# State-space decays: the causal mask added by VectorE, and growth read from the spread sums

## The chip, the cores and the metric

The kernel runs on one core of a Trainium2 chip. The metric is the device time of one execution in microseconds (us), the median of several runs. The engines work side by side, each through its own queue in a fixed order, and wait for one another on semaphores: TensorE (PE, products into PSUM; its weight loads are PEld), VectorE (DVE), ScalarE (ACT), GpSimd (POOL) and SyncE (SP), which issues most of the transfers.

## What is computed

One layer of a hybrid decoder for 336 tokens (256 new prompt tokens, 64 sampled tokens of 8 sequences, 16 meta tokens): a gated convolution branch and a state-space (SSD) branch that share one input projection, then a mixer that picks experts. The change touches the SSD branch alone, and there these two lines:

```python
acs = jnp.cumsum(dtc * Ag, axis=1)
seg = acs[:, :, None] - acs[:, None, :]
decay = jnp.exp(jnp.where(causal[None, :, :, None, None], seg, -jnp.inf))
...
y_diag = jnp.einsum('btsgr,bsgrp->btgrp', cb[..., None] * decay, dx)
y_off = jnp.einsum('btgn,bgrpn->btgrp', Cc, hc) * jnp.exp(acs)[..., None]
```

`decay` is a masked exponential of differences of running sums, for each of 32 heads; `exp(acs)` is what is called growth below.

## The kernel before

The input projection is 80 blocks of 128 output rows. Each block (`pj`) is 24 products of 320 or 336 columns: 16 with the rounded weights `wh` (made by ACT, L243) and 8 with the remainder `wl` (made by POOL, now and then by DVE, L247). The 32 heads form 8 groups `g` of four. While PE works through the projections of group g+1, the state-space work of group g (`ssd`) is let in between them, a step after each projection. PE's products are pinned to program order (`mm`, `tr`); DVE, ACT and POOL are put in order by a scheduler, except that all ACT functions that need a table are chained in program order (`chain`).

Four tiles of PSUM matter. Tag `y` has two buffers and holds in turn `pdec` (running sums of one head, spread over 128 partitions), and later `py` and `po` (the outputs). A `pdec` can be written only when the tile two before it has been read. Tag `pb` (one buffer) holds `pcv`, the sum of the long convolution: 31 taps, each one DVE instruction on 256 columns and one on 64 (L509), put at low priority so that they fill DVE's free time. Tag `pj` has three buffers, `misc` two.

In a group, `ssd` runs in steps. First `decay(0)`, `decay(1)`; after a projection `turn(0)` (transposes `ptr`, copied by ACT L643 and scaled by DVE L644 into `xt`), `decay(2)`, `decay(3)`; after the next `turn(1)`, `turn(2)`, `growth(0)`, `growth(1)`; then `inner` (L657, scores times decay), states and outputs. `update` adds to the sampled states `st` (L709) and stands just ahead of the next group's `decay(0)`. `gated` turns a projection into the convolution's input: a sigmoid on ACT (`xnf`, L219), then DVE writes `ccat` (L591 to L593), then ACT starts the sum `pcv` (L507), then DVE's taps begin.

A decay before: PE spreads the sums of head h by a product with a column of `id3`, adds the mask `mneg` by a second product with an identity, and ACT takes the exponential in three pieces, since the bias (minus the sum at the row) differs between them. Growth is spread again, two heads side by side on 64 partitions each, and ACT takes its exponential into `e2`.

Of the kernel before, what the change touches and what calls it, by code (L numbers as in the profile page):

```python
# [7 lines left out]
F32 = mybir.dt.float32  # L8
F32R = mybir.dt.float32r
BF = mybir.dt.bfloat16  # L10
# [3 lines left out]
AF = mybir.ActivationFunctionType  # L14
OP = mybir.AluOpType
# [8 lines left out]
T = TP + NQ * TS  # L24
NB_IN = 80
H = 32
# [9 lines left out]
T2 = 320  # L36
# [122 lines left out]
def body(tc, ia, oa, stop=None):  # L159
    nc = tc.nc  # L160
    with ExitStack() as top:
# [13 lines left out]
        def mm(*a_, **kw):  # L175
            i_ = nc.tensor.matmul(*a_, **kw)  # L176
            if pin[0]:
                tc.keep_in_program_order(i_)
# [28 lines left out]
        def C(name, rows=128):  # L207
            o, n = CST[name]
            if o < NCK:
                return cst[:rows, o:o + n]  # L210
            return cstm[0][:rows, o - NCK:o - NCK + n] if o < NCM else cstm[1][:rows, o - NCM:o - NCM + n]
# [228 lines left out]
        def step_sizes():  # L440
# [33 lines left out]
            act(el, p3, AF.Exp)  # L474
            acs.extend(at_[:, i] for i in range(3))
            wd.extend(wt_[:, i] for i in range(3))
            acs3 = mp.tile([3 * H, T], BF, name="acs3", tag="acs3")
            stack3(acs3, pT, H, dp, "r1")
            id3 = mp.tile([3 * H, H], BF, name="id3")
            keep(nc.vector.tensor_copy(id3, C("sel32", 3 * H)))  # L480
            mneg = mp.tile([128, T], BF, name="mneg")
            keep(nc.vector.tensor_copy(mneg, mnf))
            identb = mp.tile([128, 128], BF, name="identb")
            keep(nc.vector.tensor_copy(identb, ident))
            fixed.extend((acs3, id3, mneg, identb))
            yield

        MCAT = MC + TP + NQ * (MC + TS)
# [121 lines left out]
        def ssd(g, xg, bc, sz):  # L610
# [8 lines left out]
            def decay(r):  # L619
                h = 4 * g + r  # L620
                pb = ps.tile([128, T], F32, name="pdec", tag="y", bufs=2)[:, :T2]
                mm(pb, id3[:, h:h + 1].to_broadcast([3 * H, 128]), acs3[:, :T2], start=True, stop=False)
                mm(pb, identb, mneg[:, :T2], start=False, stop=True)
                for i, (t0, L) in enumerate(OTILES):
                    act(dec[:, r, t0:t0 + L], pb[:, t0:t0 + L], AF.Exp, bias=acs[i][:, h:h + 1])

            def growth(b):
                pb = ps.tile([128, T], F32, name="pdec", tag="y", bufs=2)[:, :T2]
                for r in range(2):
                    h = 4 * g + 2 * b + r  # L630
                    mm(pb[r * 64:(r + 1) * 64], id3[:, h:h + 1].to_broadcast([3 * H, 64]), acs3[:, :T2],
                       start=True, stop=True)
                act(e2[:, b], pb, AF.Exp)

            def decay_b(q):
                return el[:, q, 4 * g:4 * g + 4, None].to_broadcast([128, 4, P])
# [82 lines left out]
            yield  # L719
            turn(1)  # L720
            turn(2)
            growth(0)
            growth(1)
            for s_ in range(2):
                nc.scalar.copy(cz[:, 4 * s_:4 * s_ + 4, 8 * s_:8 * s_ + 8],
                               CT[:, SQ + 32 * s_:SQ + 32 * s_ + 32].rearrange("p (q t) -> p q t", q=4))
# [34 lines left out]
        def gnorm_stats():  # L761
            r8 = tp.tile([128, T], F32, name="rs", bufs=2)[:G, :T2]
            rstd_of(r8, pgn, 256, tp, load=False)
            r24 = mp.tile([3 * H, T], BF, name="acs3", tag="acs3")[:, :T2]
            nc.vector.memset(r24, 0.0)
            stack3(r24, r8, G, tp, "yo")
            return r24

        def gnorm(g, r24):
            p = ps.tile([128, T], F32, name="pgb", tag="y", bufs=2)[:, :T2]  # L770
            mm(p, id3[:, g:g + 1].to_broadcast([3 * H, 128]), r24, start=True, stop=True)
            for b in range(2):
                y = ygf[g][:, b, :T2]
                nc.vector.scalar_tensor_tensor(y, y, V("m_norm", 2 * g + b), p, op0=OP.mult, op1=OP.mult)
# [87 lines left out]
        for n, f in enumerate(conf(0) + zsteps[:1] + steps + zsteps[1:]):  # L862
            f()
            if n in (1, 4, 5):
                run(old, 1)
        acs3, id3, mneg, identb = fixed
        dt_scope.close()
        sp = ls.enter_context(tc.tile_pool(name="sp", bufs=1))

# [783 lines left out]
```

## Time and profile before

| | |
|---|---|
| median of 3 runs | 1304.52 us (1301.46 to 1305.58) |
| the profiled execution | 1300.87 us, its span 1299.1 us |
| instructions | 23902 |
| DVE, ACT, POOL busy | 74%, 41%, 46% of the span |
| products `pdec` with `acs`, `id` / with `mneg`, `identb` | 64 / 32 |
| ACT exponentials `dec` from `pdec` / `e` from `pdec` | 96 / 16 |
| first and last `pdec` product | 54.1 and 348.0 us |

In a timeline row stand the start in us, the duration, the engine, the line, the operation, output and input with the size, how many, and in brackets the idle time of the engine ahead of it with what ended it. Rows of several instructions give the time from the first start to the last end; each instruction's own duration overlaps the next by about 0.1 us on DVE and ACT and by half on PE, so costs are taken from starts. The view of windows gives for each stretch the busy time of PE, PEld, DVE, ACT and POOL with counts, then the granted TensorE clock, the DMA share and GB/s.

### The profile page before, as it was taken

To read this page: it belongs to the slowest core of one execution; us is meant where nothing else is said; L and a number is where in the kernel's file an instruction comes from. 1 tells how busy PE (TensorE), PEld (TensorE's weight loads), DVE (VectorE), ACT (ScalarE), POOL (GpSimd) and SP (SyncE) were. 2 spreads that over 40 slices of the span, in tenths; PEclk is the share of its full clock that TensorE was granted. 3 is DMA by queue.
4 is the path that set the end of the run, shared out by engine and by line. 5 is a ranking of instruction groups with operands and counts; after the bars stand their busy time and mean duration, and the time that the engine had idled before them with its cause. 6 is when DMAs were issued, how large, how long until landed. Compare 5 with 4: busy or idle time off the path is not lost.

```text
span 1299.1 us, 23902 instructions
## 1 busy us (share of the span) xinstructions
PE 1270.9 (98%) x9015; PEld 1223.2 (94%) x9015; DVE 956.2 (74%) x2240; ACT 529.6 (41%) x1395; POOL 592.9 (46%) x552
## 2 busy tenths in 40 slices
PE   9999999999989999999999899999999999999997
PEld 7998988999889999999999889999999999999997
DVE  7888778878887235549999968688788888545444
ACT  6787877888766444544232212212110110100102
POOL 2487777877774666974132223223332322122210
PEclk9899999999999999999999989999999999999999
DMA  6435453454433444766989999999999999999992
GB/s 246 165 126 185 155 191 134 156 186 167 149 129 136 146 149 153 254 231 221 382 328 416 416 414 415 414 412 408 413 414 415 415 415 414 402 414 415 405 414 88
DMA packets 85907, 373.80 MB, mean 288 GB/s; under 512 B 10000, under 2 KB 15376, under 8 KB 66208
## 3 DMA queue, kind: packets, MB, share of 16 engines
q1 hardware_dynamic: 48336, 166.82, 34.5%
q0 software_dynamic: 19584, 142.62, 26.9%
q10 hardware_dynamic: 17872, 62.84, 12.1%
q8 instruction: 71, 1.16, 0.4%
q14 instruction: 44, 0.36, 0.1%
HBM read 359.18 MB, written 13.06 MB: 287 GB/s over the span
## 4 chain that ended last, share of the span: by engine, by line
PE 83%; DVE 7%; DMA 6%; ACT 3%; issue 1%; POOL 1%; ACTq 0%; DVEq 0%
PE pj L176 32%; PE va L1517 25%; PE pj L1415 17%; DMA wuv<-in_peer_uv_dram,gid 3%; DMA eraw<-in_uT_dram 3%; PE pg L1443 1%; PE pst L176 1%; DVE ygat L1313 1%; PE po L176 1%; DVE wuv L1303 1%; PE pdec L176 1%; PE psc L1193 1%; PE py L176 1%; DVE pcv L509 1%; DMA wdt<-in_w_dt_dram 1%
## 5 line engine op out<-in xcount | busy, mean ns | idle before, releaser
L1147 POOL DMA_INDIRECT wuv<-in_peer_uv_dram,gid x136 | 173.0, 1272 | 484.7 <-PE va L1517 149.6
L247 POOL TENSOR_TENSOR wl<-wraw,wh 128x1024 fp32r<-128x1024 f32 (+1 forms) x160 | 279.6, 1760 | 117.1 <-ACT wh L243 68.8
L1517 PE MATMUL va<-S,eraw 128*128 128x184 f32 x2048 | 325.4, 320 | 0.0
L1517 PEld LDWEIGHTS va<-S,eraw 128*128 128x128 f32 x2048 | 318.9, 190 | 0.9 <-issue 0.9
L1415 PE MATMUL pj<-nd,eraw 128*128 128x184 f32 x1792 | 294.5, 324 | 9.9 <-DMA eraw<-in_uT_dram 8.1
L1415 PEld LDWEIGHTS pj<-nd,eraw 128*128 128x128 f32 x1792 | 282.8, 192 | 11.3 <-issue 9.0
L1313 DVE SCALAR_TENSOR_TENSOR ygat<-wuv,scg,ygat 128x1024 f32<-128x1024 f32 x128 | 164.1, 1282 | 108.1 <-ACT scg L1308 108.0
L176 PE MATMUL pj<-ah,wh 128*128 128x336 f32 (+1 forms) x768 | 242.5, 326 | 0.3 <-ACT xnf L219 0.3
L176 PE MATMUL pj<-al,wh 128*128 128x336 f32 (+1 forms) x768 | 232.2, 315 | 0.0
L1305 ACT ACTIVATE scg<-scg 128x1 f32<-128x1 f32 x136 | 27.3, 202 | 398.0 <-DVE wuv L1303 220.4
L1303 DVE SCALAR_TENSOR_TENSOR wuv<-wuv,x2m 128x1024 f32<-128x1024 f32 x128 | 156.2, 1220 | 17.3 <-DMA wuv<-in_peer_uv_dram,gid 17.0
L509 DVE SCALAR_TENSOR_TENSOR pcv<-ccat,vec,pcv 128x256 f32<-128x256 f32 x464 | 150.1, 389 | 17.1 <-ACT pcv L507 17.1
L243 ACT CAST wh<-wraw 128x1024 fp32r<-128x1024 f32 x125 | 131.2, 1050 | 73.4 <-PE pj L176 54.0
L176 PEld LDWEIGHTS pj<-ah,wh 128*128 128x128 f32 x768 | 145.4, 190 | 6.3 <-issue 2.0
L176 PEld LDWEIGHTS pj<-al,wh 128*128 128x128 f32 x768 | 145.0, 190 | 0.8
L176 PE MATMUL pj<-ah,wl 128*128 128x336 f32 (+1 forms) x768 | 137.2, 314 | 0.3 <-POOL wl L247 0.3
L176 PEld LDWEIGHTS pj<-ah,wl 128*128 128x128 f32 x768 | 119.8, 188 | 0.7 <-POOL wl L247 0.6
L1417 ACT ACTIVATE S<-pj 128x184 f32<-128x184 f32 x128 | 38.8, 318 | 128.0 <-PE pj L1415 127.7
L523 DVE SCALAR_TENSOR_TENSOR pj<-mcat,vec,pj 128x360 f32<-128x360 f32 x96 | 57.0, 595 | 0.6 <-ACT pj L521 0.6
L1454 DVE SCALAR_TENSOR_TENSOR S<-pg,S 128x232 f32<-128x232 f32 (+1 forms) x92 | 34.7, 420 | 29.8 <-PE pg L1443 29.6
L219 ACT ACT_TABLE_LOAD x38 | 48.8, 1283 | 0.7
L1415 PE MATMUL pj<-nd,pre 128*128 128x184 f32 x256 | 42.0, 319 | 0.0
(387 smaller groups left out, 1694.7 us busy)
## 6 DMA issues: line engine op xcount, KB each, us to landing
wraw<-in_w_in_dram SPq DMA_DIRECT2D x80, 512.0 KB, 3.3
eraw<-in_vE_dram SPq DMA_DIRECT2D x64, 512.0 KB, 9.5
eraw<-in_vE_dram ACTq DMA_DIRECT2D x64, 512.0 KB, 9.4
eraw<-in_uT_dram SPq DMA_DIRECT2D x60, 512.0 KB, 9.2
eraw<-in_uT_dram ACTq DMA_DIRECT2D x52, 512.0 KB, 9.9
st<-in_state_dram SPq DMA_DIRECT2D x8, 1024.0 KB, 6.9
out_ssm_s_dram<-st SPq DMA_DIRECT2D x8, 1024.0 KB, 6.3
wraw<-in_w_mo_dram SPq DMA_DIRECT2D x16, 512.0 KB, 3.2
```

The source lines that it names most:

```text
L176: i_ = nc.tensor.matmul(*a_, **kw)
L219: i_ = nc.scalar.activation(out, in_, f, **kw)
L243: (nc.vector.tensor_copy if on_dve else nc.scalar.copy)(h, src)
L247: (nc.gpsimd if on_pool else nc.vector).tensor_tensor(l[:, q:q + m], src[:, q:q + m], h[:, q:q + m].bitcast(F32), op=OP.subtract)
L509: t = nc.vector.scalar_tensor_tensor(o, i_, wv, a_, op0=OP.mult, op1=OP.add)
L523: nc.vector.scalar_tensor_tensor(o, cat[:, w:w + n], wv, o, op0=OP.mult, op1=OP.add)
L1147: i_ = nc.gpsimd.indirect_dma_start(out=u, out_offset=None, in_=ia["peer_uv"], in_offset=bass.IndirectOffsetOnAxis(ap=gid[:, c:c + 1], axi ...
L1303: nc.vector.scalar_tensor_tensor(u[:, :D], u[:, :D], 1.0, x2m if c < NPICK else x2e, op0=OP.mult, op1=OP.mult, accum_out=w)
L1313: nc.vector.scalar_tensor_tensor(a_, u[:, D:], scg[:, c:c + 1], a_, op0=OP.mult, op1=OP.add)
L1415: i_ = nc.tensor.matmul(p[:, :ND], raw[:, k, :], nd[:, k, :], start=(k == 0), stop=(k == KD - 1))
L1417: nc.scalar.activation(Sv(b), p[:, :ND], AF.Gelu)
L1517: i_ = nc.tensor.matmul(va[k // 2][:, k % 2], raw[:, k, :], Sv(b), start=(b == 0 and k % 2 == 0), stop=(b == 127), skip_group_check=True)
```

## The change

The product with the mask goes, and `identb` with it. DVE adds the bias and the mask in one instruction for each of the three pieces (from `pdec` in PSUM to `dec` in SBUF, without the exponential). ACT takes growth, the exponential of the sums alone, from 64 partitions of the same `pdec`, and after each second head one exponential over both heads of `dec`, in place. `growth` and its products go. `id3` and `acs3` get 128 rows instead of 96, the added ones zero.

```diff
-            acs3 = mp.tile([3 * H, T], BF, name="acs3", tag="acs3")
+            acs3 = mp.tile([128, T], BF, name="acs3", tag="acs3")
+            nc.gpsimd.memset(acs3[3 * H:], 0.0)
             stack3(acs3, pT, H, dp, "r1")
-            id3 = mp.tile([3 * H, H], BF, name="id3")
-            keep(nc.vector.tensor_copy(id3, C("sel32", 3 * H)))
+            id3 = mp.tile([128, H], BF, name="id3")
+            keep(nc.vector.tensor_copy(id3, C("sel32")))
...
-            identb = mp.tile([128, 128], BF, name="identb")
-            keep(nc.vector.tensor_copy(identb, ident))
-            fixed.extend((acs3, id3, mneg, identb))
+            fixed.extend((acs3, id3, mneg))
...
             def decay(r):
                 h = 4 * g + r
                 pb = ps.tile([128, T], F32, name="pdec", tag="y", bufs=2)[:, :T2]
-                mm(pb, id3[:, h:h + 1].to_broadcast([3 * H, 128]), acs3[:, :T2], start=True, stop=False)
-                mm(pb, identb, mneg[:, :T2], start=False, stop=True)
+                mm(pb, id3[:, h:h + 1].to_broadcast([128, 128]), acs3[:, :T2], start=True, stop=True)
                 for i, (t0, L) in enumerate(OTILES):
-                    act(dec[:, r, t0:t0 + L], pb[:, t0:t0 + L], AF.Exp, bias=acs[i][:, h:h + 1])
-
-            def growth(b):
-                pb = ps.tile([128, T], F32, name="pdec", tag="y", bufs=2)[:, :T2]
-                for r in range(2):
-                    h = 4 * g + 2 * b + r
-                    mm(pb[r * 64:(r + 1) * 64], id3[:, h:h + 1].to_broadcast([3 * H, 64]), acs3[:, :T2],
-                       start=True, stop=True)
-                act(e2[:, b], pb, AF.Exp)
+                    nc.vector.scalar_tensor_tensor(dec[:, r, t0:t0 + L], pb[:, t0:t0 + L], acs[i][:, h:h + 1],
+                                                   mneg[:, t0:t0 + L], op0=OP.add, op1=OP.add)
+                hs_ = slice(r % 2 * 64, r % 2 * 64 + 64)
+                act(e2[hs_, r // 2], pb[hs_], AF.Exp)
+                if r % 2:
+                    act(dec[:, r - 1:r + 1], dec[:, r - 1:r + 1], AF.Exp)
...
             turn(1)
             turn(2)
-            growth(0)
-            growth(1)
```

The rows that follow show the order of instructions, with the engines each waits for. They are of group 4 (of 0 to 7; `pdec` at 216.79 us in the profile), unless it is said otherwise. `pst` is what `update` added, `cbuf` the last tap of the convolution, `pgn` a sum of squares, `e` is `e2`. A semaphore that carries the name of an engine is raised by that engine.

PE, the second pair of decays, between two projections, before:

```order
L181 MATMUL ptr<-cst,spr 128x128 x3
L176 LDWEIGHTS id_594 [waits PE_49]
L176 MATMUL pdec<-acs_585,id_594 128x320 [waits Activation_49]
L176 LDWEIGHTS identb
L176 MATMUL pdec<-mneg,identb 128x320
L176 LDWEIGHTS id_594 [waits PE_49]
L176 MATMUL pdec<-acs_585,id_594 128x320 [waits Activation_49]
L176 LDWEIGHTS identb
L176 MATMUL pdec<-mneg,identb 128x320
L176 MATMUL pj<-ah,wh 128x336 [waits DVE_49]
```

and now:

```order
L181 MATMUL ptr<-cst,spr 128x128 x3
L176 LDWEIGHTS id_595
L176 MATMUL pdec<-acs_585,id_595 128x320 [waits Activation_49]
L176 LDWEIGHTS id_595
L176 MATMUL pdec<-acs_585,id_595 128x320 [waits Activation_49]
L176 MATMUL pj<-ah,wh 128x336
```

Two products of four are left; both still wait for ACT, which before meant the three exponentials of the head two earlier, and now means the growth of that head.

DVE at the same place, from the state updates on, now (before, no row of L623 stood there, and three pairs of taps followed the state updates, the `cbuf` pair among them):

```order
L704 TENSOR_TENSOR st<-st,pst_2898 128x512 [waits PE_49]
L623 SCALAR_TENSOR_TENSOR dec<-pdec,acs,mneg 128x64 [waits PE_49]
L623 SCALAR_TENSOR_TENSOR dec<-pdec,acs,mneg 128x128 x2
L623 SCALAR_TENSOR_TENSOR dec<-pdec,acs,mneg 128x64 [waits PE_49]
L623 SCALAR_TENSOR_TENSOR dec<-pdec,acs,mneg 128x128 x2
...
L508 SCALAR_TENSOR_TENSOR cbuf<-ccat,vec,pcv 128x64 [waits DVE_49]
L751 TENSOR_TENSOR pgn<-pgn 8x320 [waits PE_49]
L623 SCALAR_TENSOR_TENSOR dec<-pdec,acs,mneg 128x64 [waits PE_49]
L623 SCALAR_TENSOR_TENSOR dec<-pdec,acs,mneg 128x128 x2
L639 TENSOR_TENSOR xt_2971<-ptr,dtok_498 128x256 [waits Activation_49]
L623 SCALAR_TENSOR_TENSOR dec<-pdec,acs,mneg 128x64 [waits PE_49]
L623 SCALAR_TENSOR_TENSOR dec<-pdec,acs,mneg 128x128 x2
```

The first six stand behind all four state updates, with four pairs of taps behind them, of which one moved there from ahead of the updates; the other six stand ahead of `ccat`.

ACT there, now:

```order
L219 ACT_TABLE_LOAD [waits DVE_49]
L219 ACTIVATE e_2915<-pdec 64x320 [waits PE_49]
L219 ACTIVATE e_2915<-pdec 64x320 [waits DVE_49,PE_49]
L219 ACTIVATE dec<-dec 128x640
L243 CAST wh<-wraw 128x1024 [waits DMAHW0_49,PE_49]
...
L219 ACTIVATE e_2915<-pdec 64x320 [waits DVE_49,PE_49] x2
L219 ACTIVATE dec<-dec 128x640
L243 CAST wh<-wraw 128x1024 [waits DMAHW2_49,PE_49,Pool_49]
L219 ACT_TABLE_LOAD
L219 ACTIVATE xnf<-pj,vec 128x336 [waits PE_49]
```

Each growth waits for DVE's three additions on the same `pdec`, and in groups 1, 2, 4 and 6 the load of the exponential's table stands behind the first of these waits; in groups 0, 3, 5 and 7 it stands ahead of it. A second load of that table, which stood between `xnf` and the old growth, is gone. In the whole program 49 table loads become 42.

In group 6 one remainder `wl` is made by DVE, as before, and stands there now between the two halves:

```order
L623 SCALAR_TENSOR_TENSOR dec<-pdec,acs,mneg 128x64 [waits PE_49]
L623 SCALAR_TENSOR_TENSOR dec<-pdec,acs,mneg 128x128 x2
L508 SCALAR_TENSOR_TENSOR pcv<-ccat,vec,pcv 128x64 [waits DVE_49]
L508 SCALAR_TENSOR_TENSOR cbuf<-ccat,vec,pcv 128x256 [waits DVE_49]
L508 SCALAR_TENSOR_TENSOR cbuf<-ccat,vec,pcv 128x64 [waits DVE_49]
L247 TENSOR_TENSOR wl<-wraw,wh 128x1024 [waits PE_49,DMAHW0_49,Activation_49,Pool_49]
L751 TENSOR_TENSOR pgn<-pgn 8x320 [waits PE_49]
L623 SCALAR_TENSOR_TENSOR dec<-pdec,acs,mneg 128x64 [waits PE_49]
```

It waits for ACT's `wh`, which on ACT stands right behind the exponential of the first two heads, as the `CAST` in the rows of group 4 does.

More of the change, by code (lines that the diff above doesn't have):

```diff
@@ L763, in gnorm_stats @@
             rstd_of(r8, pgn, 256, tp, load=False)
-            r24 = mp.tile([3 * H, T], BF, name="acs3", tag="acs3")[:, :T2]
+            r24 = mp.tile([128, T], BF, name="acs3", tag="acs3")[:, :T2]
             nc.vector.memset(r24, 0.0)
@@ L770, in gnorm @@
             p = ps.tile([128, T], F32, name="pgb", tag="y", bufs=2)[:, :T2]
-            mm(p, id3[:, g:g + 1].to_broadcast([3 * H, 128]), r24, start=True, stop=True)
+            mm(p, id3[:, g:g + 1].to_broadcast([128, 128]), r24, start=True, stop=True)
             for b in range(2):
@@ L865, in body @@
                 run(old, 1)
-        acs3, id3, mneg, identb = fixed
+        acs3, id3, mneg = fixed
         dt_scope.close()
```

## The prediction

> **What bounds the kernel.** I read the page's engines and chain first, then a table of windows, then the timelines of PE, DVE and ACT around one group's decays.
>
> ```profile
> PE 1270.9 (98%) x9015; PEld 1223.2 (94%) x9015; DVE 956.2 (74%) x2240; ACT 529.6 (41%) x1395; POOL 592.9 (46%) x552
> PE 83%; DVE 7%; DMA 6%; ACT 3%; issue 1%; POOL 1%; ACTq 0%; DVEq 0%
> 270.00:330.00 60.00, 60.00 (x443) 55.40 (x442) 51.66 (x146) 48.87 (x137) 47.25 (x53) 1.00 0.46 169
> 330.00:390.00 60.00, 56.47 (x409) 50.79 (x409) 49.11 (x94) 42.91 (x86) 44.58 (x33) 0.97 0.38 132
> 450.00:510.00 60.00, 60.00 (x411) 59.99 (x410) 25.03 (x25) 26.45 (x36) 37.60 (x16) 1.00 0.42 143
> 1050.00:1120.00 70.00, 70.00 (x563) 69.48 (x562) 54.80 (x92) 7.46 (x30) 16.32 (x13) 1.00 1.02 414
> ```
>
> PE is the bound nearly everywhere. The decays lie between 54 and 348 us; there PE has no free microsecond, but DVE is busy for 51.66 of 60 and ACT for 48.87, so each is close behind. From 345 to 386 PE has gaps (56.47 of 60). Behind that PE is full again (450 to 510, 1050 to 1120; the late transfers start as PE frees buffers), so I carry any shift at 386 us to the end one for one.
>
> **What PE loses.** Group 4, PE:
>
> ```profile
> 216.79 0.31 PE L176 MATMUL pdec<-acs,id 96*128 96x320 bf16 x1
> 216.93 0.30 PE L176 MATMUL pdec<-mneg,identb 128*128 128x320 bf16 x1
> ...
> 221.93 0.30 PE L176 MATMUL pdec<-acs,id 96*128 96x320 bf16 x1
> ...
> 222.38 0.42 PE L176 MATMUL pj<-ah,wh 128*128 128x336 f32 x1
> ...
> 226.92 0.46 PE L176 MATMUL pdec<-acs,id 96*64 96x320 bf16 x4
> 227.31 0.43 PE L176 MATMUL pj<-ah,wh 128*128 128x336 f32 x1
> ```
>
> A mask product starts 0.14 us after the one ahead of it: 4 of them are 0.56. The four growth products take 227.31 - 226.92 = 0.39. That is 0.95 us in a group and 7.6 in eight, if nothing else waits. The wider `id3` (96 to 128 rows) costs nothing: both row counts stand above with 0.30. The setup's changes (one POOL memset more, one copy of `identb` less) lie beside PE's work.
>
> **What DVE and ACT get.** The same group, DVE, then ACT:
>
> ```profile
> 213.65 4.76 DVE L509 SCALAR_TENSOR_TENSOR pcv<-ccat,vec,pcv 128x256 f32<-128x256 f32 x16
> 218.31 0.69 DVE L709 TENSOR_TENSOR st<-st,pst 128x512 f32<-128x512 f32 x1
> 218.91 0.49 DVE L509 SCALAR_TENSOR_TENSOR pcv<-ccat,vec,pcv 128x256 f32<-128x256 f32 x1
> 219.30 0.69 DVE L709 TENSOR_TENSOR st<-st,pst 128x512 f32<-128x512 f32 x1
> 219.90 0.29 DVE L509 SCALAR_TENSOR_TENSOR pcv<-ccat,vec,pcv 128x64 f32<-128x64 f32 x1
> 220.09 1.29 DVE L709 TENSOR_TENSOR st<-st,pst 128x512 f32<-128x512 f32 x2
> 221.28 1.27 DVE L509 SCALAR_TENSOR_TENSOR pcv<-ccat,vec,pcv 128x256 f32<-128x256 f32 x4
> ...
> 228.88 0.48 DVE L591 SCALAR_TENSOR_TENSOR ccat<-pj,vec,xnf 128x256 f32<-128x256 f32 x1 [4.69 <-ACT xnf L219]
> ...
> 232.47 3.01 DVE L509 SCALAR_TENSOR_TENSOR pcv<-ccat,vec,pcv 128x256 f32<-128x256 f32 x10 [2.12 <-ACT pcv L507]
> ```
>
> ```profile
> 216.74 1.28 ACT L219 ACT_TABLE_LOAD   x1
> 218.03 1.55 ACT L219 ACTIVATE dec<-pdec,acs 128x64 f32<-128x64 f32 x6
> 220.03 1.05 ACT L243 CAST wh<-wraw 128x1024 fp32r<-128x1024 f32 x1 [0.45 <-PE pj L176]
> ...
> 224.33 0.71 ACT L732 ACTIVATE Bm<-xt,cstm 128x128 f32<-128x128 f32 x2
> ...
> 228.30 0.54 ACT L219 ACTIVATE xnf<-pj,vec 128x336 f32<-128x336 f32 x1
> ...
> 229.18 1.28 ACT L219 ACT_TABLE_LOAD   x1
> 230.48 0.77 ACT L219 ACTIVATE e<-pdec 128x320 f32<-128x320 f32 x2
> ```
>
> From starts, a tap of 256 columns costs 0.39 (218.91 to 219.30), one of 64 costs 0.19 (219.90 to 220.09), a state update 0.60 (218.31 to 218.91). The new addition on 128 columns is not in the trace; as a line through 64 and 256 it costs 0.26, and a head 0.19 + 2 x 0.26 = 0.71. Bounds: all three at 0.19 (0.57) or at 0.39 (1.17). I take 0.71, since the taps are the same instruction with one input in PSUM. Four heads are 2.84 us a group, 22.7 in eight. DVE has room for that: it stands idle 4.69 ahead of `ccat` and 2.12 ahead of the taps. Growth costs ACT 0.33 (half of 0.77, less the overlap); the exponential over 640 columns lies between that and the cast of 1024 (1.05), and I take 0.65. ACT drops 1.28 + 0.65 = 1.93 between `xnf` and `pcv`, so taps start 3.59 - 1.93 = 1.66 after `ccat`, with one more wait between engines about 1.75.
>
> **The stall, group 4.** PE may write the third `pdec` when ACT has read the first for growth, and ACT may do that when DVE has added. DVE comes to the state updates one pair of taps (0.58) earlier, at 217.73, and needs 4 x 0.60 + 0.39 + 0.19 + 0.71 to the end of the first head: 221.42; second head 222.13. The table load stands behind the first wait: 221.42 + 1.28 = 222.7, growth 223.05 and 223.4. PE wants the third spread at 221.93 - 0.28 = 221.65, gets it at about 223.1, the fourth at 223.5, and resumes projections at 223.65 where it did at 222.49 (222.38 and 0.11 of overlap). So 0.28 + 0.28 saved become 1.16 lost; with growth's products gone, 0.77 is left. Without the load behind the wait (groups 3, 5, 7) the second head's growth decides, some 0.6 earlier.
>
> What is queued behind on ACT: the cast to `wh` of 220.03 moves to 224.2 and ends 225.3; PE needs that weight at 227.31, POOL's `wl` 2.4 later, so this stays covered by about 2 us. DVE's second half: four pairs of taps 2.33 from 222.13, `pgn` 0.40, head three to 225.6, `xt` 0.33, head four to 226.65. ACT: cast 225.3, copies for `ccat`, `xt` and three `Bm` (0.71 for two) about 1.5 to 226.8, growth twice 227.45, exponential 228.1, cast 229.1, table 230.4, `xnf` 230.95. So `ccat` comes about 2.1 late and the taps start at 232.8, 0.3 later than 232.47.
>
> **All groups.** Counted in the same way, DVE's start of taps against before is: group 0 about -1.45 (below), group 1 +0.5, group 2 -1.1 and group 3 -1.65 (more taps stand behind the additions there, so these come sooner), group 4 +0.3, group 5 0.0, and group 6 +2:
>
> ```profile
> 302.15 1.23 DVE L247 TENSOR_TENSOR wl<-wraw,wh 128x1024 fp32r<-128x1024 f32 x1
> ...
> 308.28 0.48 DVE L591 SCALAR_TENSOR_TENSOR ccat<-pj,vec,xnf 128x256 f32<-128x256 f32 x1 [4.19 <-ACT xnf L219]
> ...
> 311.88 3.02 DVE L509 SCALAR_TENSOR_TENSOR pcv<-ccat,vec,pcv 128x256 f32<-128x256 f32 x10 [2.11 <-ACT pcv L507]
> ```
>
> There DVE's `wl` (302.15 before) waits for a cast behind ACT's first exponential (303.4 load, 304.1 growths, 304.75, cast 305.75), so it ends at 306.95, head four at 309.1, `xnf` at 312.1, taps at 313.85. A lead does not add up without end: state updates cannot start before PE's products, which end at 216.8 in group 4 against DVE's 218.31, so it stays near -1.5 from group 3 on; group 6 makes it +0.4. In group 0 PE waited for ACT's exponentials:
>
> ```profile
> 58.03 1.35 ACT dec L219 x5
> 59.38 0.04 issue
> 59.42 0.43 PE pdec L176 x2
> 59.86 2.18 PE pj L176 x14
> ```
>
> Now two growths at 57.8 (load ahead of the wait) free both by 58.5 and PE resumes at 58.8: 1.06 gained, and 0.39 with growth's products, -1.45.
>
> Behind group 7 comes a chain between DVE and ACT:
>
> ```profile
> 345.15 3.31 DVE L824 TENSOR_TENSOR cbuf<-cbuf,rs 128x320 f32<-128x320 f32 x8 [2.33 <-ACT rs L822]
> ```
>
> DVE was free for 2.33 ahead of it; 2.84 of additions fill that, then ACT's growth, exponential and `rs` (0.35 + 0.65 + 0.4) follow: about +1.85. The old growth of 0.77 at 348.9 no longer stands between ACT's squares, so +1.1. Sum: +0.4 + 1.1 = **+1.5 us** on 1300.87, 1302.4 for such an execution. The median stands 3.65 above the profiled run, so 1306.0.
>
> **A rule against it.** PE's new gaps may cost clock:
>
> ```profile
> 368.52 0.70 PE L176 MATMUL pst<-wx,xt 128*128 128x256 f32 x2 [2.15 <-DVE dec L657]
> 369.00:372.00 3.00, 3.00 (x22) 2.52 (x21) 3.00 (x9) 3.00 (x7) 1.11 (x1) 0.56 0.11 45
> ...
> 814.54 2.73 PE L1415 MATMUL pj<-nd,eraw 128*128 128x184 f32 x16 [2.87 <-DMA eraw<-in_uT_dram]
> 814.00:816.00 2.00, 1.46 (x9) 1.49 (x10) 1.40 (x3) 0.50 (x2) 1.19 (x1) 1.00 1.01 412
> ```
>
> A gap of 2.15 us was followed by a clock of 0.56 over 3 us, one of 2.87 by none. [...] I take nothing, and keep the loss as a rival.
>
> **Rivals.** (a) Faster: the scheduler's order brings DVE's additions just behind the state updates, so where DVE comes in time PE waits little. If each group kept its 0.95 and group 0 its 1.45, less 1.1 in the tail, -7; with half of it, -4 to -5: about 1300. For it speak groups 2 and 3; against it, that DVE reaches the updates 1.5 us after PE's products. (b) Slower, by price: at 0.90 a head a group is 0.76 dearer on DVE, the leads of groups 0 to 3 shrink, and the same count ends at +3.9 behind group 6 and +5.8 behind the tail: 1310.3; at the upper bound, 1.17 a head, it ends near +14: 1318.9. It decides from about 0.83 a head, where the sum passes 3.9. For it speaks that DVE is 86% busy here, against it the taps' price. (c) Slower, by clock: stalls beyond about 2.1 us that halve the clock for 3 us cost 1.3 + 0.4 each; in four groups +6.8: 1312.8. (d) The products stay in the program: the rows of order exclude it.
>
> **Numbers.** Forecast, within a few us of before, 0.48; (a) 0.20; (b) 0.18; (c) 0.14. A measurement of this kernel can tell some 0.3%, 3.9 us, from no change: faster 0.20, within 0.48, slower 0.32. The range runs from (a) with most of its gain, 1298, past (b) at 0.90 and (c), with some added waits, to 1316.
>
> **What would show it.** Right: PE's third and fourth `pdec` wait for ACT `e`, 1 to 2 us, in most groups, and 32 `pdec` products are left; the additions cost near 0.26; `ccat` waits for `xnf` about 4 us still, and the wait for `pcv` falls below 1; group 6 is the longest. Wrong: `pdec` without waits and a distance between groups 0.95 shorter (a), additions near 0.4 (b), a granted clock under 1.00 between 100 and 340 us (c). A late part that runs in another order by a few us would make the sum wrong with each step right.

## The result, and the profile after

| | before | after |
|---|---|---|
| median | 1304.52 us (7 runs, 1301.46 to 1306.61) | 1313.76 us (7 runs, 1309.42 to 1317.69) |
| the profiled execution, its span | 1300.87, 1299.1 us | 1313.32, 1311.5 us |

The ratio is 1.007, with a 95% interval of 1.0053 to 1.0087: the changed kernel is slower by 0.7%, 9.2 us. The two profiled executions lie 12.4 us apart; 3.2 of that is that the one of before lies that much further below its median.

The page of the changed kernel, engines and chain:

```profile
PE 1267.3 (97%) x8951; PEld 1223.0 (93%) x8951; DVE 982.6 (75%) x2335; ACT 517.1 (39%) x1324; POOL 592.0 (45%) x553
...
PE 76%; DVE 13%; DMA 6%; ACT 3%; issue 1%; POOL 0%; ACTq 0%; DVEq 0%; SPq 0%; POOLq 0%
```

PE has 64 instructions less and is busy 3.6 us less, in a span that is 12.4 longer. The share of PE on the chain fell from 83% to 76%, and DVE's rose from 7% to 13%: PE now waits for a chain that runs through DVE.

The stretch that counts runs from the first `pdec` of group 0 to the first of group 7. The view of windows of before, for that stretch (the first number behind the colon is its length, the next PE's busy time):

```profile
54.13:336.95 282.82, 281.39 (x2066) 257.21 (x2064) 232.28 (x665) 226.70 (x618) 219.62 (x233) 1.00 0.46 167
```

And of after:

```profile
54.19:347.87 293.68, 277.17 (x2010) 255.96 (x2008) 252.65 (x746) 214.74 (x554) 217.64 (x233) 0.99 0.45 161
```

Length less busy time is PE's idle time: 1.43 us before, 16.51 after. PE is busy 4.2 us less and idle 15.1 more, which makes the 10.9 us by which group 7 comes late. The view of PE's waits of after for the same stretch (in total, how often, the longest) names them:

```profile
PE pdec L176 <- ACT e L219: 13.3, 13, 3.7
PE pq L176 <- DVE xt L639: 2.3, 3, 1.1
PE ptr L181 <- DVE xt L639: 0.7, 1, 0.7
```

The timeline of PE, after, has them one by one (in brackets the wait and what ended it):

```profile
98.03 0.45 PE L176 MATMUL pdec<-acs,id 128*128 128x320 bf16 x2
104.23 0.30 PE L176 MATMUL pdec<-acs,id 128*128 128x320 bf16 x1 [1.17 <-ACT e L219]
104.69 0.30 PE L176 MATMUL pdec<-acs,id 128*128 128x320 bf16 x1 [0.16 <-ACT e L219]
...
146.98 0.30 PE L176 MATMUL pdec<-acs,id 128*128 128x320 bf16 x1 [1.76 <-ACT e L219]
...
230.07 0.30 PE L176 MATMUL pdec<-acs,id 128*128 128x320 bf16 x1 [1.98 <-ACT e L219]
...
322.33 1.07 PE L176 MATMUL pq<-st,gs 128*32 128x256 f32 x16 [1.15 <-DVE xt L639]
...
347.87 0.45 PE L176 MATMUL pdec<-acs,id 128*128 128x320 bf16 x2
...
382.56 0.70 PE L176 MATMUL pst<-wx,xt 128*128 128x256 f32 x2 [2.72 <-DVE dec L652]
...
400.57 0.81 PE L176 MATMUL pgn<-sq,cstm 128*128 128x320 f32 x2 [0.78 <-POOL sq L742]
```

and the same places of before (no wait of 0.3 us or more stood at a `pdec` behind group 0):

```profile
93.98 0.31 PE L176 MATMUL pdec<-acs,id 96*128 96x320 bf16 x1
...
336.95 0.31 PE L176 MATMUL pdec<-acs,id 96*128 96x320 bf16 x1
...
386.81 0.81 PE L176 MATMUL pgn<-sq,cstm 128*128 128x320 f32 x2 [1.07 <-POOL sq L749]
```

So behind group 0 the third `pdec` of a group waits 0.79 to 1.98 us for growth; it is longest in groups 1, 2, 4 and 6 (1.17, 1.76, 1.98, 1.81), where the table load stands behind the wait for DVE, and 0.8 in 3, 5 and 7, where it stands ahead of it.

### The profile page after: what moved, and what is told of

It reads as the page before. It is cut to its first block, busy times and chain, and to the rows that moved or that the text cites. A ratio compares the mean times of both kernels' runs of the same rounds, so it can differ in the third digit from the quotient of the medians.

```text
span 1311.5 us, 23814 instructions
## 1 busy us (share of the span) xinstructions
PE 1267.3 (97%) x8951; PEld 1223.0 (93%) x8951; DVE 982.6 (75%) x2335; ACT 517.1 (39%) x1324; POOL 592.0 (45%) x553
## 4 chain that ended last, share of the span: by engine, by line
PE 76%; DVE 13%; DMA 6%; ACT 3%; issue 1%; POOL 0%; ACTq 0%; DVEq 0%; SPq 0%; POOLq 0%
PE pj L176 26%; PE va L1510 24%; PE pj L1408 19%; DVE pcv L508 5%; DMA eraw<-in_uT_dram 4%; DMA wuv<-in_peer_uv_dram,gid 2%; PE pg L1436 2%; DVE pj L522 1%; DVE st L704 1%; DVE dec L623 1%; PE psc L1186 1%; ACT L219 1%; DMA wdt<-in_w_dt_dram 1%; PE pst L176 1%; PE pq L176 1%
## 5 line engine op out<-in xcount | busy, mean ns | idle before, releaser
L176 PE MATMUL pj<-ah,wh 128*128 128x336 f32 (+1 forms) x768 | 245.3, 330 | 0.4 <-ACT xnf L219 0.4
L522 DVE SCALAR_TENSOR_TENSOR pj<-mcat,vec,pj 128x360 f32<-128x360 f32 x96 | 56.4, 588 | 3.3 <-ACT pj L520 3.0
```

Of the source, the lines that this page charges most:

```text
L522: nc.vector.scalar_tensor_tensor(o, cat[:, w:w + n], wv, o, op0=OP.mult, op1=OP.add)
```

## Group 0, where the largest part went

Group 0 lasts from 54.19 to 98.03, 43.84 us, against 39.85 before. DVE there, after (the last row is of the chain behind group 7, and is used further below):

```profile
54.54 1.51 DVE L623 SCALAR_TENSOR_TENSOR dec<-pdec,acs,mneg 128x64 f32<-128x64 f32 x6 [0.35 <-PE pdec L176]
55.96 0.67 DVE L508 SCALAR_TENSOR_TENSOR pcv<-ccat,vec,pcv 128x64 f32<-128x64 f32 x2
56.54 0.59 DVE L522 SCALAR_TENSOR_TENSOR pj<-mcat,vec,pj 128x360 f32<-128x360 f32 x1
...
358.46 1.70 DVE L817 TENSOR_TENSOR cbuf<-cbuf,rs 128x320 f32<-128x320 f32 x4 [1.32 <-ACT rs L815]
```

and before:

```profile
54.62 0.59 DVE L523 SCALAR_TENSOR_TENSOR pj<-mcat,vec,pj 128x360 f32<-128x360 f32 x1
```

The last instruction of the short convolution, which makes the input of `bc`, now stands behind the first six additions, 1.92 us later. ACT, after:

```profile
57.17 1.05 ACT L243 CAST wh<-wraw 128x1024 fp32r<-128x1024 f32 x1 [2.91 <-PE pj L176]
...
58.34 1.28 ACT L219 ACT_TABLE_LOAD   x1
59.63 0.58 ACT L219 ACTIVATE bc<-pj 128x256 f32<-128x256 f32 x3
60.08 0.54 ACT L219 ACTIVATE sz<-pj,vec 128x320 f32<-128x320 f32 x1
60.63 1.28 ACT L219 ACT_TABLE_LOAD   x1
61.92 0.89 ACT L219 ACTIVATE e<-pdec 64x320 f32<-64x320 f32 x2
```

A cast that stood behind the exponentials before now stands ahead of both table loads, `bc` and `sz`; growth starts at 61.92, although the additions it needs ended at 56.05. PE waits 3.75 us for it, and then the clock falls, as the windows of after show (the third number from the end is the granted clock):

```profile
64.00:68.00 4.00, 4.00 (x23) 3.98 (x22) 3.62 (x14) 3.47 (x9) 0.61 (x1) 0.78 0.02 4
...
148.00:152.00 4.00, 4.00 (x18) 4.00 (x18) 2.54 (x10) 3.95 (x11) 2.84 (x2) 0.61 0.66 263
...
232.00:236.00 4.00, 4.00 (x30) 3.99 (x29) 1.49 (x6) 3.92 (x10) 3.74 (x4) 1.00 0.76 288
```

From the end of the `pdec` products to the end of the 24 products of the projection behind them it took 4.86 us at 63.29 and 5.24 at 147.73, against 3.72 in the other groups before group 7: 1.14 and 1.52 lost, in groups 0 and 2.

**The books to group 7**: waits for `pdec` 13.36 (3.75 in group 0, 9.61 in groups 1 to 6), for `xt` 2.99, slow clock 2.66; less the products saved, 7 x 0.95 = 6.65, and less the waits that before had there (0.27, 0.56, 0.59): 10.94. Measured, 347.87 - 336.95 = 10.92.

## The experiments

Theories: PE's stall behind the readers of `pdec` and the order in group 0 make the loss; the rival is that DVE's load does, wherever the additions stand. Each kernel was timed beside before on the same chip. "Stretch" is the time from the first `pdec` of group 0 to that of group 7, "to `pgn`" the part behind it, both from the profiled execution; the waits are those inside the stretch. Before itself took 1303.1 to 1304.5 us on the several chips, so two kernels are compared by their distance from the before beside them.

| kernel | median, that of before (us) | ratio, 95% | stretch | PE idle in it | waits for `pdec` | for `xt` | DVE busy | to `pgn` |
|---|---|---|---|---|---|---|---|---|
| before | | | 282.82 | 1.43 | 0.3 | 0 | 82% | 49.86 |
| after | 1313.76, 1304.52 | 1.007 (1.0053 to 1.0087) | 293.68 | 16.51 | 13.3 | 3.0 | 86% | 52.70 |
| short_first | 1312.15, 1304.31 | 1.0068 (1.0047 to 1.0089) | 289.69 | 13.87 | 12.0 | 1.9 | 87% | 53.18 |
| load_early | 1310.62, 1304.31 | 1.0054 (1.0034 to 1.0073) | 287.10 | 11.30 | 10.3 | 1.0 | 88% | 54.17 |
| growth_first | 1307.59, 1304.31 | 1.0027 (1.0014 to 1.0041) | 286.63 | 11.02 | 8.3 | 2.7 | 89% | 55.10 |
| own_growth | 1313.79, 1304.31 | 1.0078 (1.0059 to 1.0097) | 291.11 | 10.46 | 7.0 | 0.7 | 87% | 53.24 |
| load_only | 1312.11, 1303.17 | 1.0072 (1.005 to 1.0095) | 288.28 | 6.06 | 0.3 | 5.2 | 97% | 52.28 |
| load_taps | 1314.27, 1303.08 | 1.0084 (1.0066 to 1.0102) | 290.96 | 6.50 | 0.2 | 4.3 | 89% | 52.68 |
| gf_misc | 1302.37, 1303.17 | 0.999 (0.9973 to 1.0006) | 280.97 | 7.59 | 3.8 | 3.4 | 91% | 53.84 |
| mid_new | 1305.7, 1303.17 | 1.0024 (1.0009 to 1.0039) | 287.52 | 12.04 | 7.1 | 4.1 | 88% | 50.24 |
| best | 1297.92, 1303.08 | 0.9965 (0.9949 to 0.9981) | 278.53 | 5.33 | 2.4 | 2.3 | 91% | 50.24 |
| best_dvx | 1296.03, 1303.08 | 0.995 (0.9932 to 0.9969) | 278.25 | 4.64 | 2.8 | 1.0 | 92% | 49.77 |
| before_tidy | 1302.18, 1303.86 | 0.9984 (0.9973 to 0.9995) | 282.89 | 1.29 | 0.7 | 0 | 84% | 49.80 |

From `pgn` to the end of the span it took 911.0 (after) to 915.7 us (before_tidy), 912.3 in before. This part, which the change hardly touches (`gnorm` reads the wider `id3` there), scatters over some 5 us, so a difference of one or two microseconds in the time says less than one in a stretch.

### short_first: the order in group 0 alone

In `decay`, where `short` holds the name of the last L522:

```diff
-                    nc.vector.scalar_tensor_tensor(dec[:, r, t0:t0 + L], pb[:, t0:t0 + L], acs[i][:, h:h + 1],
-                                                   mneg[:, t0:t0 + L], op0=OP.add, op1=OP.add)
+                    a_ = nc.vector.scalar_tensor_tensor(dec[:, r, t0:t0 + L], pb[:, t0:t0 + L], acs[i][:, h:h + 1],
+                                                        mneg[:, t0:t0 + L], op0=OP.add, op1=OP.add)
+                    if g == 0 and r < 2:
+                        tc.add_manual_dep(a_.ins, short[0], mybir.DependencyInfo(mybir.DependencyClass.NoSync,
+                                                                               mybir.DependencyReason.DATA), reason="short first")
```

> The changed kernel, with one order fixed: in group 0 the additions of heads 0 and 1 stand behind the last instruction of the short convolution on VectorE (L522), as the exponentials did before. Theory (order in group 0): the six additions ran ahead of that instruction (54.54 to 56.05 against 56.54), so bc, sz and the two table loads came late on ACT and PE waited 3.75 us for e and then ran 4 us at a clock of 0.79. With the order fixed bc, sz come about 2 us earlier; PE's wait for the third pdec falls from 3.75 to 1 to 2 us, the clock between 60 and 64 us is above 0.95, the first pdec of group 1 comes at 94.5 to 96 us instead of 98.03, and the time falls by 2 to 4 us, to about 1310 to 1312. Rival (VectorE's 22.7 us of additions are the cost, wherever they stand): group 1 may come earlier, but later groups lose it again and the time stays within 1 us of the changed kernel, 1313.8.

The timeline of PE, short_first:

```profile
60.33 0.30 PE L176 MATMUL pdec<-acs,id 128*128 128x320 bf16 x1 [1.71 <-ACT e L219]
...
94.64 0.45 PE L176 MATMUL pdec<-acs,id 128*128 128x320 bf16 x2
```

The wait fell from 3.75 to 1.71, the clock between 60 and 64 stayed at 1.00, and group 0 lasts 40.52 instead of 43.84; group 7 comes 4.1 us earlier than in after. So the order in group 0 is shown to be the cause of 3.3 us there. The time, 7.8 us above before instead of 9.2, is not told apart from that of after: the part behind `pgn` was 1.8 longer in this execution. The cast is still ahead of the second table load (57.14), so growth starts at 59.85, not at the 57.8 of the prediction.

### load_early: the table load not behind the wait

```diff
             def decay(r):
                 h = 4 * g + r
+                if r == 0:
+                    chain(nc.scalar.preload_act_table_set("natural_log_exp_and_others"))
```

> The changed kernel with the load of the exponential's table asked for ahead of the first spread of each group, so that it does not stand behind the wait for VectorE in groups 1, 2, 4 and 6. Theory (the load behind the wait is the larger part of the stall there): the waits for the third pdec in these four groups fall from 1.17, 1.76, 1.98 and 1.81 to 0.3 to 0.9 us, groups 0, 3, 5 and 7 stay (3.75, 0.79, 0.80, 0.83), and the time falls by 3 to 5 us, to 1309 to 1311. Rival (the load is hidden by the second head's additions, as in groups 3, 5 and 7, which wait without it): waits fall by 0.3 at most and the time stays within 1.5 us of 1313.8.

The timeline of PE, load_early, group 2:

```profile
144.03 0.30 PE L176 MATMUL pdec<-acs,id 128*128 128x320 bf16 x1 [0.40 <-ACT e L219]
144.74 0.30 PE L176 MATMUL pdec<-acs,id 128*128 128x320 bf16 x1 [0.41 <-ACT e L219]
```

and the first `pdec` of groups 1 and 7:

```profile
98.19 0.45 PE L176 MATMUL pdec<-acs,id 128*128 128x320 bf16 x2
...
341.16 0.45 PE L176 MATMUL pdec<-acs,id 128*128 128x320 bf16 x2
```

The third `pdec` waits 0.59, 0.40, 0.81 and 0.79 in groups 1, 2, 4 and 6, as expected, and the waits of groups 1 to 6 together fall from 9.61 to 6.41. The load behind the wait is worth 3.2 us of these waits, and the time is in the expected range. More came with it: groups 1 to 6 take 242.97 us, against 249.84 in after and 242.97 in before. Besides the 3.2, the waits for `xt` fell by 2.0, and the slow clock in group 2 (1.5) did not come. So with all additions and still 6.4 us of waits these six groups are level with before. Group 0 stays as bad (3.75).

### growth_first: ACT reads first, DVE adds behind it

```diff
+                hs_ = slice(r % 2 * 64, r % 2 * 64 + 64)
+                act(e2[hs_, r // 2], pb[hs_], AF.Exp)
                 for i, (t0, L) in enumerate(OTILES):
...
-                hs_ = slice(r % 2 * 64, r % 2 * 64 + 64)
-                act(e2[hs_, r // 2], pb[hs_], AF.Exp)
```

> The changed kernel, with the two readers of a pdec swapped: ACT takes growth from it first, VectorE adds behind it. Theory (PE's stall is the chain state updates, additions, table load, growth): the load and growth now lie beside the state updates, so the third pdec waits only for the end of the additions. The waits of PE for its third and fourth pdec in groups 1 to 7 (1.17, 1.76, 0.79, 1.98, 0.80, 1.81, 0.83 us, and 0.16 to 0.57 for the fourth) fall to 0.5 or less together in each group, they end at DVE and not at ACT; the distance between groups shrinks by 1 to 1.5 us, group 0 gains 2 to 3, and the time falls by 7 to 11 us, to about 1303 to 1307. Rival (VectorE's load is the cost): waits move to another place, the time stays within 3 us of 1313.8.

In groups 1 to 7 the third and fourth `pdec` together wait 0.4 to 1.2 us, for DVE; expected was 0.5 at most, so the wait for DVE behind the state updates is larger than I thought. Groups 1 to 6 take 243.27 us, against 249.84 after and 242.97 before. The time, 1307.6, lies just above the expected range: group 0 gained only 0.5. The timeline of DVE shows why:

```profile
50.89 2.58 DVE L259 CAST acs<-s3r 32x336 bf16<-32x336 f32 x1
```

This cast of the setup took 0.33 in before; here it holds up the short convolution, and with it `bc`.

### own_growth: the mask by DVE, growth by products as before

```diff
-                hs_ = slice(r % 2 * 64, r % 2 * 64 + 64)
-                act(e2[hs_, r // 2], pb[hs_], AF.Exp)
...
+            growth(0)
+            growth(1)
```

> One part of the change alone: the mask is added by VectorE, but growth has products and pdec tiles of its own again, at its old place. Theory (ACT behind VectorE makes the stall): PE's third and fourth pdec wait for VectorE alone; the waits fall to 0 to 0.5 us a group in groups 1 to 7, the growth products cost 0.39 us a group again (3.1 in all), and the table load between xnf and pcv is back (1.28 and 0.65 to 0.77 us a group for the taps). Together 2 to 5 us below the changed kernel, 1309 to 1312. Rival (VectorE's load is the cost): as slow as the changed kernel or slower by the 3.1 us of products, 1314 to 1317.

A miss: it is as slow as after. The waits of PE for the stretch, own_growth:

```profile
PE pdec L176 <- DVE dec L623: 7.0, 12, 0.9
PE pj L176 <- ACT bc L219: 1.3, 1, 1.3
```

Even without ACT behind it, the wait for DVE is 7.0 us in groups 1 to 6, and growth's products and its second table load are back. The mask's part of the change alone is a loss. What growth's part alone is worth no run shows.

### load_only and load_taps: DVE's load with no wait of PE

Both are the kernel before with 96 more instructions of the additions' sizes. In load_only they read the finished `dec`:

```diff
                     act(dec[:, r, t0:t0 + L], pb[:, t0:t0 + L], AF.Exp, bias=acs[i][:, h:h + 1])
+                for i, (t0, L) in enumerate(OTILES):
+                    nc.vector.scalar_tensor_tensor(idle[:, t0:t0 + L], dec[:, r, t0:t0 + L], acs[i][:, h:h + 1],
+                                                   mneg[:, t0:t0 + L], op0=OP.add, op1=OP.add)
```

> The kernel before, and 96 more additions on VectorE of the same sizes at the same places (they read the finished dec and write a tile that nobody reads), so that VectorE has the load of the change while no product of TensorE waits for it. Theory (it is PE's wait for readers of pdec that costs, not VectorE's load): PE's pdec products wait no more than before (0.3 us in all), the first pdec of group 7 comes within 2 us of 336.95, the last part loses 1 to 2 us, and the time is 1304 to 1307. Rival (VectorE's load is the cost): the lateness at group 7 is 6 us or more, and the time is 1310 to 1315.

The groups of DVE by form, load_only (busy time, mean of one in ns):

```profile
L628 DVE SCALAR_TENSOR_TENSOR idle<-dec,acs,mneg 128x128 f32<-128x128 f32 x56 | 30.7, 576 | 0.0
L628 DVE SCALAR_TENSOR_TENSOR idle<-dec,acs,mneg 128x64 f32<-128x64 f32 x28 | 22.2, 794 | 1.2 <-ACT dec L219 1.2
```

Group 7 came 5.5 us late and the time is one that the rival named. But with all operands in SBUF one took 0.58 and 0.79 us on average, the small ones longer than the large: the load was about twice that of the change (0.34 and 0.27), so this run could not decide. In load_taps the third operand is the sum in PSUM, and the instructions stand between the taps:

```diff
+                if w in (6, 12, 18, 24):
+                    for n_ in (64, 128, 128):
+                        nc.vector.scalar_tensor_tensor(lt_[:, :n_], cat[:, w + NM:w + NM + n_], wv, acc[:, :n_], ...)
```

> The kernel before, with 96 more instructions on VectorE of the same sizes and, this time, with one operand in PSUM as the additions have (they read the sum of the convolution between its taps and write a tile that nobody reads). In load_only the extra additions lay in SBUF alone and took 0.58 and 0.79 us each beside GpSimd instead of 0.34 and 0.27, so that the load was twice that of the change. Theory (VectorE's load at its true price is mostly hidden): each extra instruction takes 0.27 to 0.34 us, PE's waits for xt come to less than 2 us over groups 1 to 6, the first pdec of group 7 comes at 337 to 339 us, and the time is 1303 to 1307. Rival (the load itself costs what load_only lost): first pdec of group 7 at 341 or later, time 1309 or more.

The waits of PE for the stretch, load_taps:

```profile
PE ptr L181 <- DVE xt L649: 2.9, 4, 1.6
PE pq L176 <- DVE xt L649: 1.4, 2, 0.7
PE pcb L176 <- DVE dec L662: 1.2, 2, 0.6
```

One took 0.35 and 0.28, the change's price, no `pdec` waited, and still group 7 came 8.2 us late and the kernel is as slow as after. The rival holds here: DVE had no room for 2.84 us a group in the kernel before. Groups 0 and 1 lose nothing yet (39.84 and 40.23 us, against 39.85 and 40.95); the loss comes in groups 2 to 6, as waits for what DVE makes late and, in group 6, a slower clock (0.83 between 312 and 322 us) behind a wait of 1.65. It is not the change's own case, though: here DVE still waits 12.2 us for `pcv` between 54 and 345 us, while the change frees ACT (taps start 1.89 us behind `ccat` in groups 2, 4, 5 and 6, 1.90 in 3, against 3.59 to 3.60 in groups 1 to 6 of before), so that these waits fall from 16.3 us (groups 0 to 6 of before) to 3.8. The runs below have the load and the relief.

### gf_misc: the stall taken away, the load kept

From growth_first, with another buffer for the third head:

```diff
-                pb = ps.tile([128, T], F32, name="pdec", tag="y", bufs=2)[:, :T2]
+                pb = ps.tile([128, T], F32, name="pdec", **(dict(tag="misc", bufs=2) if r == 2 else dict(tag="y", bufs=2)))
```

> As growth_first (1307.6), and the third pdec of each group takes a PSUM buffer of misc, so that it waits for no reader, and the fourth waits for the additions of the first head alone. Theory (the rest of the stall, 0.57 and 0.40 us a group, is the wait for VectorE behind the state updates): both waits fall to 0.2 or less in groups 1 to 7, the distance between groups comes to 39.2 to 39.6 us, about 0.8 below that of before, and the time falls by 4 to 6 us, to 1301.5 to 1303.5. Rival (VectorE's load): the waits come back at xt or ccat, the distance stays above 40 us and the time within 2 us of 1307.6.

The third `pdec` waits no more and the fourth 0.46 at most in groups 1 to 6, which take 239.97 us, 3.0 less than before. With the full load the kernel is level with before, where after was 9.2 us above. The distances, 39.13 to 40.75 us, are not all the 39.2 to 39.6 expected: groups 1, 3 and 5 are the long ones. What is left in these groups is mostly the wait of `pq` (2.7 us of 5.1 in all). The timeline of ACT in group 5, gf_misc:

```profile
260.34 0.74 ACT L219 ACTIVATE dec<-dec 128x640 f32<-128x640 f32 x1 [3.98 <-DVE dec L625]
260.98 1.03 ACT L243 CAST wh<-wraw 128x1024 fp32r<-128x1024 f32 x1
...
267.50 0.54 ACT L219 ACTIVATE xnf<-pj,vec 128x336 f32<-128x336 f32 x1
267.94 0.42 ACT L638 COPY xt<-ptr 128x128 f32<-128x128 f32 x2
```

and of PE:

```profile
269.28 1.07 PE L176 MATMUL pq<-st,gs 128*32 128x256 f32 x16 [1.16 <-DVE xt L639]
```

ACT stands 3.98 us before the exponential of the first two heads, all that follows on ACT comes later, `xnf` and the copies of `ptr` with it. `pq` does not read `xt`, but takes a buffer of `misc` that a `ptr` held, so it waits until ACT has copied this `ptr` and DVE, behind ACT, has scaled it. The cast to `wh` stands behind that exponential in groups 1, 3 and 5; in 2, 4 and 6 the scheduler put it ahead, so that ACT makes it during the wait, and these groups take 39.1 to 39.6 us.

### mid_new: groups 0 and 7 by products

From gf_misc; `decay_old` and `growth` are those of before:

```diff
             def decay(r):
+                if g in (0, G - 1):
+                    return decay_old(r)
...
             turn(1)
             turn(2)
+            if g in (0, G - 1):
+                growth(0)
+                growth(1)
```

> As gf_misc in groups 1 to 6; groups 0 and 7 take the mask and growth by products, as before. Theory (in group 0 the chain over bc, sz and two table loads, and behind group 7 the chain of VectorE and ACT, are where the additions can't be hidden): group 0 is back at 39.9 us, groups 1 to 6 take 39.2 to 39.6 each, the part behind group 7 takes as long as before (386.81 - 336.95 = 49.9, within 1.5), and the time is 3 to 6 us below before: 1298.5 to 1301.5. Rival (VectorE's load): 1304 or more.

A miss in the time (1305.7, where 1298.5 to 1301.5 was expected and 1304 or more was the rival's sign), and half a miss in its parts. Behind group 7 it took 50.24, as expected: the additions there are what lengthens that part. Groups 1 to 6 take 243.32 us, no less than in before, though their code is that of gf_misc. Here the cast to `wh` stands behind the first exponential in groups 1, 2, 4 and 6, ACT stands idle 4.1 to 4.5 us before it, and these take 40.8 to 41.5 us; in 3 and 5 the cast is ahead, the idle time is 2.2, and they take 39.5. So in gf_misc and mid_new the place of this one cast goes with 1 to 2 us of a group's length; that it is the cause is not shown, since no run moved the cast alone. Group 0, though computed as before, lasts 44.2, and PE waits there 2.2 us for `identb` and 2.1 for exponentials. The timeline of DVE, mid_new:

```profile
50.56 2.57 DVE L259 CAST acs<-s3r 32x336 bf16<-32x336 f32 x1
...
53.51 2.36 DVE L485 CAST identb<-cst 128x128 bf16<-128x128 f32 x1
```

and of POOL:

```profile
50.54 2.39 POOL L247 TENSOR_TENSOR wl<-wraw,wh 128x1024 fp32r<-128x1024 f32 x1 [2.93 <-ACT wh L243]
...
53.28 2.51 POOL L247 TENSOR_TENSOR wl<-wraw,wh 128x1024 fp32r<-128x1024 f32 x1
```

Both casts started just behind a remainder of POOL and ended within 0.2 us of it. In before the first started at 50.35 and POOL's at 50.92, and it took 0.33.

### best and best_dvx: what was found, put together

best is gf_misc with group 7 by products; `id3`, `mneg` and `identb` are made ahead of `stack3`, whose last cast goes to ACT:

```diff
-            stack3(acs3, pT, H, dp, "r1")
+            stack3(acs3, pT, H, dp, "r1", last=nc.scalar.copy)
```

best_dvx has this in `turn` besides:

```diff
-                nc.scalar.copy(x_[:, 256:], p[:, 256:])
+                (nc.vector.tensor_copy if i else nc.scalar.copy)(x_[:, 256:], p[:, 256:])
```

> As gf_misc (1302.4), with two things mended. Group 7 takes mask and growth by products as before. The constants id3, mneg and identb are made before the running sums are split, and the last cast of the split is done by ACT, since in growth_first, own_growth, gf_misc and mid_new this cast on VectorE (0.33 us in before) started beside a GpSimd instruction and took 2.5. Theory (these two places are what gf_misc still gives back): from the first pdec of group 0 to that of group 1 39.5 to 40.2 us (41.0 in gf_misc), from that of group 7 to pgn 49.5 to 51 (52 to 55 in the runs with the additions there), time 1297 to 1300.5. Rival (the loss only moves on to the next stage): 1302 or more.

> As best, and in turn(1) and turn(2) VectorE, which there stands idle 3.6 us for xnf, copies the third part of ptr in place of ACT. Theory (what is left in groups 1 to 6 of gf_misc, 3.4 us in all, is PE's pq waiting for xt, which waits for ACT's copies, which stand behind an exponential held up by the additions): these waits go, the distances between groups 1 and 7 come to 39.1 to 39.6 each, and the time is 2 to 3.5 us below that of best: 1294 to 1298. Rival (xt waits for VectorE's load): the waits stay and the time is that of best.

The stretch and the waits of best_dvx:

```profile
52.75:331.00 278.25, 273.61 (x2009) 252.19 (x2007) 256.35 (x764) 212.63 (x541) 218.58 (x236) 1.00 0.48 172
```

```profile
PE pdec L176 <- DVE dec L629: 2.8, 5, 1.0
PE ptr L181 <- DVE xt L659: 1.0, 2, 0.7
```

Group 0 of best lasts 38.94 us, less than expected, and group 7 to `pgn` takes 50.24. The times are in the expected ranges; best_dvx's waits for `xt` fell to 1.0, not to nothing, three of its six distances (39.9, 40.1 and 40.5) lie above the 39.6 expected, and its gain over best (1.9 us) is just under the 2 expected and lies within the intervals of the two. DVE is busy 92% of the stretch, with the full load of seven groups' additions, and PE is idle 4.6 us: the load can be carried where the waits of PE behind it are kept short.

### before_tidy: the side edits without the change

The kernel before, with the two edits of best_dvx to `stack3` and `turn`, and the constants made earlier.

> The kernel before, with only the two side edits of best_dvx: the constants made ahead of the split with its last cast on ACT, and in turn(1), turn(2) the copy of the third part of ptr by VectorE. The mask and growth stay products. Theory (what makes best_dvx faster is the change itself, with its waits taken away, 0.95 us of PE a group): in the kernel before neither edit touches a wait of PE, since the cast took 0.33 us and no pq waited for xt; the distances between groups stay at 39.9 to 41.4 us and the time within 2 us of before, 1301 to 1306. Rival (the side edits are the gain): distances of 39.5 or less, time 1296 to 1299.

It is 0.16% below before (0.05 to 0.27%), with the distances of before and a stretch of 282.89. So by themselves the side edits bring some 1.7 us, of which the stretch shows nothing, and the rest of best_dvx's 7 comes from the change in seven groups with most of its waits taken away.

## Why the forecast came out too low

The forecast, 1306.0, took +1.5 us and "within 0.3%" as the likeliest; the measured +9.2 lies in the range and with the cases of the slower sign. That the range holds it is partly luck: its upper half was drawn for rivals (b) and (c), while the largest miss, group 0, stood in none of them. By its own terms, on the profiled executions:

| term | predicted | measured |
|---|---|---|
| group 0 | -1.45 | +4.0 |
| groups 1 to 6 | +1.85 (to +0.4 behind group 6) | +6.9, of it 1.5 clock |
| behind group 7, to `pgn` | +1.1 | +2.8 |
| the rest | 0 | -1.3, within its scatter |
| sum | +1.5 | +12.4 |

- **Prices: right but for one.** The additions cost 0.71 us a head by starts (62.87 to 63.58 us), the exponential of 640 columns 0.65 by starts, as taken, 32 products are left, and each group saves 0.95 on PE. Growth is dearer: one of 64 partitions takes 0.44 by starts, where 0.33 was taken from those of 128 partitions. Rival (b) falls by the price, and (a) by the waits, which came in every group.
- **The stall: right in kind and size.** The third and fourth `pdec` wait for ACT `e`, 1.0 to 2.1 us together in groups 1 to 6 (about 1.7 counted for group 4, 2.14 measured), longer where the load stands behind the wait. load_early, growth_first and gf_misc take it away piece by piece: 9.61 us, then 6.4, 5.2 and 1.4.
- **Group 0: the step that failed most.** "Now two growths at 57.8 (load ahead of the wait) free both by 58.5 and PE resumes at 58.8" took ACT's order of before. I had worked out what the additions do to the work behind them, but not to the short convolution's instruction that they were put ahead of. short_first shows 3.3 us of the 5.5; best, with growth ahead of the additions, lasts 38.94, so -0.9 was to be had there.
- **Groups 1 to 6: a wrong measure.** I counted DVE's start of taps and let a lead make good what PE lost. But the length is PE's busy time and its idle time, and PE's own sum was there: in group 4, 1.16 lost in place of 0.56 saved, 0.77 net of growth's products; measured +1.8. The wait of `pq` and `ptr` for `xt`, 3.0 us, was not foreseen; in gf_misc it comes from ACT held up by the additions, and best_dvx, which takes two of the copies from ACT, has 1.0 of it left. "DVE has room for that" is refuted for the kernel before by load_taps; with the change, load_early shows six groups that carry the load in the time of before.
- **Behind group 7: right in kind, too small.** The chain over `rs` starts 10.59 us behind group 7's first `pdec` (358.46) against 8.20, +2.4 where +1.85 was said; mid_new and best, without additions there, give it back.
- **The clock: "I take nothing" cost 2.7 us.** Rival (c) was true in two groups of the seven in the stretch, though not by its bound of 2.1 us: a gap of 1.76 was followed by a clock of 0.61, one of 1.98 by 1.00. That gaps as short as those counted here cost no clock, as the zero has it, no run shows; the runs showed 1.14 us lost in group 0, behind a gap of 3.75, and 1.52 in group 2, behind that of 1.76. What decides is open; no run was made for it.
- **"Right if" lines**: the waits, the price and the short wait for `pcv` (0.54 a group) came; that group 6 is the longest did not (42.62 us; group 0 43.84, group 2 42.66). "A granted clock under 1.00 between 100 and 340 us" came too.

Left open: how much of the loss in groups 1 to 6 the load alone would have made. Stall and load don't simply add: load_taps, with the load alone, came 8.2 us late to group 7, and after, with the load and 9.61 us of waits for `pdec` in groups 1 to 6, lost 6.9 there; that the stall gives DVE time to catch up is my estimate from these. Open too: whether ACT's cast alone, put ahead of the exponential in every group, would bring what best_dvx brought.

## What to carry to other kernels

Count a change on the engine that bounds, as busy time and idle time, place by place; a lead of another engine pays only if a wait of the first one ends with it. Before a step is moved to a nearly full engine, look in its new order at what it is put ahead of, in the first and last rounds of the loop above all, where other work stands beside it. The saving (here 0.95 us of products a group) can be had without most of the wait that costs, if the reader that is free comes first and the next writer has another buffer (gf_misc: 3.8 us of waits for `pdec` in the stretch, 13.3 in after).

## What was not expected of the hardware

In mid_new two DVE casts with all operands in SBUF, started during a POOL instruction, lasted about until that one ended: 2.57 us (the last cast of `acs`) and 2.36 (`identb`), where POOL's had started 0.02 and 0.23 earlier and ended 0.20 and 0.08 earlier; in before they took 0.33 and 0.22. The cast of `acs` took 2.5 to 2.6 us in four of the kernels. A start inside a POOL instruction is not enough: `identb` in before began 0.11 behind one and took 0.22. The 96 instructions of load_only, all operands in SBUF, took 0.26 to 2.49 us each, half of them 0.34 or less; that the long ones stood beside POOL's is my estimate from the two casts. Those of load_taps, with one operand in PSUM, took 0.35 and 0.28 on average, while POOL was busy for 218.46 of the stretch's 290.96 us. In mid_new, where group 0 is computed as before, that group came out 4.3 us longer, with PE's waits of 2.2 for `identb` and 2.1 for exponentials; the cast of `acs` had started 0.2 us later than in before, and the remainder 0.4 earlier. What makes one such cast long and another short no run shows.

The granted clock after a wait of PE does not follow the length of the wait alone: 0.61 after 1.76 us and 0.78 after 3.75 in after, but 1.00 after 1.98 there and after 2.49 in group 0 of gf_misc.
